# A two-layer conformer and attention trunk: the first layer's gated channels move one step ahead of queries and keys

## The chip, the cores and the metric

The kernel runs on one core of one Trainium2 chip. Its time is the device time of one execution in microseconds. Before the change three executions took 1055.93, 1056.01 and 1057.12 us; the median is 1056.01 us. One more execution was profiled: it took 1054.58 us, of which 1052.8 us lie between the first and the last instruction.

## The reference

Two layers work on 256 latent tokens and 256 context tokens of width 1024. Only the token-mixing half of the first layer matters here. Cut to that:

```python
h, hc = modulate(rmsnorm(x)), modulate(rmsnorm(xc))
p, pc = h @ w_in, hc @ w_in            # columns: GLU a | GLU g | q | k | v | gates
# convolution branch, 512 channels
u = a * sigmoid(g)
u = dwconv1d(u, dw, dw_b)              # 31 taps, each channel for itself
y_conv = silu(layernorm(u)) @ w_conv_out
# attention, 8 heads of 64: latent queries see a window of latent keys and all context keys,
# context queries see the context keys alone
y_attn = merge_heads(softmax(q @ k.T * scale + bias) @ v) @ w_na_out
# gated sum, and the residual add
x = x + g1 * ((sigmoid(p_gate_c) * y_conv + sigmoid(p_gate_a) * y_attn) @ w_out)
```

In the first layer the context tokens go through all of it too; in the second only their keys and values are needed.

## The kernel before

**Storage and matmuls.** Activations lie transposed: channels on the 128 partitions, tokens along the free axis (256 latent, then 256 context). Every weight is split into a high part and a remainder, and so is every activation, and a product is three matmuls (`mm3`, lines 196 to 199): high by high, high by low, low by high. A weight unit is 128 by 1024 values and makes one *group*: 8 blocks of 128 by 3 matmuls, 24 matmuls of 512 columns that add up in one PSUM bank. The high part is a cast on ScalarE (ACT). The remainder is either a subtraction on VectorE (DVE, line 168) or, for the units listed in `ADDED`, a DMA that adds in flight, issued by GpSimd (POOL, line 218). There are 8 PSUM banks: 4 named `main` for groups, 2 `sc`, 1 `pt` and 1 `po` (line 72).

**Slots and side work.** `group` calls `slot()` twice in a group of 512 columns, in the middle and at the end. A slot lets each generator in the list `side` take one step. Two of them matter: `conv_run` emits `rate[0]` taps of the depthwise convolution (one DVE instruction of 128 by 512 a tap, line 673), and `Attention.run` calls `Attention.step`, which decides by its count of slots whether a part of the attention is emitted now. `conv_run` is first in the list.

**Order of instructions.** The program order is a priority. The compiler's scheduler walks through it with its own estimate of durations and puts onto each engine the earliest instruction in program order that is ready. The order on each engine is then fixed, and the engine takes its instructions strictly in that order. `issue_after` adds an edge: a tap that is emitted after the scores of an attention block stands behind the last row maximum of that block (`after`, lines 516 and 660). So the taps emitted before a block may be placed ahead of its maxima, and the later ones may not.

**The convolution.** Channels are worked in four chunks j = 0 to 3. `glu(j)` (line 687) multiplies the two GLU groups of a chunk (a tanh on ACT, line 691, and one DVE instruction, line 693) and appends its 31 taps to the list. The taps of one chunk form a chain through the accumulator `cb[j]`. After the attention, `layer_norm` (line 938) emits what is left of the taps at 5 a slot, adds the chunks (lines 949 to 951), forms the mean with a matmul five slots later (line 955), and so on.

**Queries, keys and attention.** `qk(j)` (line 843) makes a group of queries and a group of keys for a pair of heads, turns them by the rotary tables on DVE (lines 859 to 869) and splits them (881 on ACT, 882 on DVE). With each pair one latent block is queued, and with each second pair one context block. A block passes three stages: `issue` (the score matmuls, line 495, the row maxima on DVE, 516, exponentials on ACT, 519, and their scaling, 522), `turn` (transposes on TensorE, 561, copies on ACT, 564 and 567) and `values` (578 and 587). `ahead(j)` forces steps until no block with a pair up to j is waiting to be issued, and returns the last copy of a `turn` in those steps. `glu_groups(j)` (line 701) makes the two GLU groups of a chunk, calls `ahead`, and lets `glu(j)` stand behind that copy.

**Stages of the first layer around the change.** The values and chunk 0 of the convolution come first. Then line 840 sets 2 taps a slot, and the program goes through queries and keys of pair 0, and for j = 1, 2, 3 the GLU groups of chunk j and queries and keys of pair j, at 3 taps a slot from j = 2 on. Up to five gate groups (line 708, a tanh each) follow while attention is busy, then empty slots until it is done. The other gate groups come after that, with the tiles of the pool `ec`, whose storage the attention held: among them the buffers `own` for the products of the modulation rows (`ada_dots`, line 304, 48 DVE instructions of 128 by 1024 in this stage). Both output projections of the branches follow, and `w_out`.

The second layer has its own order in the same lines, chosen by `last`.

Of the kernel before, what the change touches and what calls it, by code (L numbers as in the profile page):

```python
# [53 lines left out]
def trunk(ctx: ExitStack, tc: tile.TileContext, xt, cvec, crow, wall, wada, params, bias_t, rope_t, out):  # L54
# [13 lines left out]
    def nm(s):  # L68
        uid[0] += 1
        return f"{s}_{uid[0]}"  # L70
# [3 lines left out]
    def psum(tag="main"):  # L74
        return psp.tile([P, 512], F32, tag=tag, bufs=BANKS[tag], name=nm(tag))

    def tmp(w=512):
        return tp.tile([P, w], F32, tag="t", bufs=5, name=nm("t"))
# [10 lines left out]
    def add_side(gen):  # L89
        side.append(gen)  # L90

    def slot():
        for g in list(side):
            try:
                next(g)
            except StopIteration:
                side.remove(g)
# [79 lines left out]
    def wunit(l, u, at=None, cuts=1):  # L177
        w, more = wparts(l, u, at, cuts)
        more()
        return w  # L180
# [8 lines left out]
    def back(ps):  # L189

        return ps.rearrange("p (c r) -> p r c", r=2)

    def halves(a):
        return a.rearrange("p (r c) -> p r c", r=2)
# [403 lines left out]
    def blocks(ap):  # L598
        return ap.rearrange("p (r b c) -> p b r c", r=ROWS, b=NB_)
# [32 lines left out]
    for l in range(DEPTH):  # L632
        last = l == DEPTH - 1
# [4 lines left out]
        with ExitStack() if last else start as e1a:  # L638
# [36 lines left out]
            rate = [0.0]  # L675

            def conv_run():
                due = 0.0
                while True:
                    due += rate[0]  # L680
                    while due >= 1:
                        due -= 1
                        if taps:
                            conv_tap(*taps.pop(0))
                    yield

            def glu(j, pa, pg):
                while taps and taps[0][0] <= j - NU_:
                    conv_tap(*taps.pop(0))
                sg = tmp()  # L690
                act.activation(halves(sg[:, :T]), back(pg[:, :T]), AF.Tanh, scale=0.5)
                u = us[j % NU_][:, :, PAD : PAD + S]
                dve.scalar_tensor_tensor(
                    halves(u[:, 0]) if NS == 1 else u, halves(sg[:, :T]), 1.0, back(pa[:, :T]), ALU.add, ALU.mult
                )
                taps.extend((j, t) for t in range(TAPS))

            def in_group(t, c, tag="main"):
                return group(psum(tag), unit8(l, U_IN + t), *h1, c)

            def glu_groups(j):
                pa = in_group(T_GLU + 2 * (j - 1), ALL)
                pg = in_group(T_GLU + 2 * (j - 1) + 1, ALL)
                copied = None if last else att.ahead(j - 2)
                with tc.issue_after(copied.ins) if copied else ExitStack():
                    glu(j, pa, pg)

            def gate(pool_, n):
                ps = in_group(T_GATE + n, ALL)
                g = new_gate(pool_, n)  # L710
                act.activation(halves(g), back(ps[:, :T]), AF.Tanh, scale=0.5)

            with ExitStack() as e1b:
# [3 lines left out]
                att = Attention(l, eb, T, V, VW, oh, ol, after)  # L717

                def keep_v(t, ps):
                    if t > 1:  # L720
                        act.copy(halves(V[t - 2]), back(ps))
                        return
                    v = tmp()
                    act.copy(halves(v), back(ps))
                    for b in range(NB_):
                        for r in range(2):
                            at = r * GW + BASE[b]
                            sp.dma_start(VW[2 * t + r :: ROWS, b], v[at : at + WC])  # L728
# [108 lines left out]
                    glu_groups(1)  # L837

                conv = conv_run()
                rate[0] = 3 if last else 2.0  # L840
                add_side(conv)

                def qk(j):

                    att.ahead(j - 2)
                    bt = eb.tile([P, 5, NS_ // 2], F32, tag="bias", bufs=2 if last else 1, name=nm("bias"))
                    both = []
                    for what in range(2):
                        w = T if what == 0 else 2 * S
                        sc = HD ** -0.5 if what == 0 else 1.0  # L850
                        ps = in_group((T_Q, T_K)[what] + j, slice(0, w))
                        if what == 0:
                            with tc.issue_after(lastdma[0].ins):
                                sp.dma_start(bt, bias_t[l, j])
                        r1, r2 = tmp(), tmp()
                        got = back(ps[:, :w])
                        lat, ctx_ = (got[:, 0], got[:, 1]) if w > S else (got, None)
                        part = halves if w == S else lambda a: a
                        dve.tensor_tensor(part(r1[:, LAT]), lat, part(rope[:, 0, :]), ALU.mult)
                        dve.stream_shuffle(part(r2[:, LAT]), lat, SWAP16)  # L860
                        dve.tensor_tensor(r2[:, LAT], r2[:, LAT], rope[:, 1, :], ALU.mult)
                        if what == 0:
                            rq = tmp()
                            dve.tensor_tensor(
                                rq[:, LAT].rearrange("p (b r c) -> p b r c", b=NB_, r=ROWS),
                                blocks(r1[:, LAT]), blocks(r2[:, LAT]), ALU.add,
                            )
                        else:
                            dve.tensor_tensor(r1[:, LAT], r1[:, LAT], r2[:, LAT], ALU.add)
                        f = eb.tile([P, 2, KN if what else w], F32R, tag="qk"[what], bufs=2, name=nm("qk"))  # L870
                        if what == 0:
                            to = [([f[:, a, LAT] for a in range(2)], rq[:, LAT])]
                            if T > S:
                                to.append(([f[:, a, CTX] for a in range(2)], ctx_))
                        else:
                            rv_ = r1[:, LAT].rearrange("p (r c) -> p r c", r=ROWS)
                            to = [([f[:, a, KCTX] for a in range(2)], ctx_)]
                            for d, c in ((slice(0, KL), slice(GW - TC, GW)), (slice(KX, KN), slice(0, TC))):
                                to.append(([f[:, a, d].rearrange("p (c r) -> p r c", r=ROWS) for a in range(2)], rv_[:, :, c]))
                        for (hi, lo), src in to:  # L880
                            act.activation(hi, src, AF.Identity, scale=sc)
                            end = dve.scalar_tensor_tensor(lo, src, sc, hi.bitcast(F32), ALU.mult, ALU.subtract)  # L882
                        both.append(f)
                    att.pair(j, *both, bt, end)

                if l == 0:
                    for t in range(4):
                        keep_v(t, pv[t])
                    qk(0)
                    arun = att.run()  # L890
                    add_side(arun)
                    for j in range(1, 4):
                        glu_groups(j)
                        qk(j)
                        rate[0] = 3
                else:
                    glu_groups(2)
                    rate[0] = 3
                    wvs = [wunit(l, U_V + uu) for uu in range(4)]
                    for half in range(2):  # L900
                        pv = {t: psum() for t in (2 * half, 2 * half + 1)}
                        for k in range(KD):
                            v_tile(pv, wvs[k // 2], k, pv)
                            if k % 2:
                                slot()
                        for t, p in pv.items():
                            keep_v(t, p)
                    qk(0)
                    glu_groups(3)
                    arun = att.run()  # L910
                n = 0
                if last:
                    add_side(arun)
                    for j in range(1, 4):
                        gate(ea, n)
                        n += 1
                        qk(j)
                while att.busy() and n < (14 if last else 5):
                    gate(ea, n)
                    n += 1  # L920
                while att.busy():
# [435 lines left out]
```

## Time and profile before

| | |
|---|---|
| median of three executions | 1056.01 us (1055.93 to 1057.12) |
| profiled execution | 1054.58 us |
| its span, first to last instruction | 1052.8 us |
| TensorE matmul (PE) busy | 1032.4 us, 98% |
| DVE busy | 893.2 us, 85% |
| ACT busy | 565.6 us, 54% |
| mean granted TensorE clock | 0.997 |
| last matmul of chunk 0 issued, first tap | 56.0 us, 58.6 us |
| last tap of the first layer | 211.5 us |

A line of the profile's timeline has a start, a duration, the engine, the line of the kernel, the operation, what it writes and reads, its shape and a count; in brackets stands the idle time of the engine before it and what ended that. A line of the table of stretches has, after the stretch, its length and the busy time of each engine in it. Matmuls are pipelined and their ends are modelled, so a busy PE can still lose a little between two starts.

### The profile page before, as it was taken

How to read it: one execution, taken by the hardware profiler on the slowest of the kernel's cores; microseconds unless marked ns; L12 is line 12 of the kernel's file. 1: busy time of each engine (PE TensorE's matmuls, PEld its weight loads, DVE VectorE, ACT ScalarE, POOL GpSimd, SP SyncE). 2: the span in 40 equal slices, each digit the busy share in tenths (PEclk: the TensorE clock that was granted, in tenths of full speed). 3: DMA queues.
4: the chain of work that ended last, by engine and by line, in shares of the span. 5: the costliest groups of instructions: out<-in, count | busy, mean ns of one | idle time of the engine just before them, and what ended most of it. 6: DMA issues, size and time to landing. Idle time of an engine off the chain costs nothing.

```text
span 1052.8 us, 17991 instructions
## 1 busy us (share of the span) xinstructions
PE 1032.4 (98%) x6886; PEld 932.9 (89%) x6886; DVE 893.2 (85%) x1608; ACT 565.6 (54%) x921; POOL 43.7 (4%) x59
## 2 busy tenths in 40 slices
PE   9999999999999999999999999999999999999997
PEld 7787788888889988888888889999889999999996
DVE  6568899999998787878788888799899988988883
ACT  4458768545434644444444223545777666766652
POOL 1111110011000000000000000000000000000000
PEclk9999999999999999999999999999999999999998
DMA  9989674888945345454545887556734485666781
GB/s 374 305 221 229 156 181 121 258 255 236 305 146 177 104 140 160 140 164 143 166 145 160 301 289 249 180 189 209 208 123 135 161 292 176 193 201 199 221 283 57
DMA packets 59511, 209.26 MB, mean 199 GB/s; under 512 B 7201, under 2 KB 7457, under 8 KB 59425
## 3 DMA queue, kind: packets, MB, share of 16 engines
q1 hardware_dynamic: 54384, 190.77, 55.3%
q0 software_dynamic: 4752, 17.30, 8.7%
q8 instruction: 54, 0.88, 0.3%
q14 instruction: 33, 0.26, 0.1%
q10 hardware_dynamic: 288, 0.04, 0.0%
HBM read 187.63 MB, written 1.05 MB: 179 GB/s over the span
## 4 chain that ended last, share of the span: by engine, by line
PE 68%; DVE 17%; ACT 5%; DMA 4%; issue 3%; SPq 1%; DVEq 0%; ACTq 0%
PE main L197 20%; PE main L198 20%; PE main L199 20%; DVE cb L673 6%; PE main L736 4%; DVE wlo L168 3%; DMA raw<-in_wall 2%; DVE t L304 2%; DMA own<-in_wada 1%; SPq L728 1%; PE sc L197 1%; PE sc L199 1%; PE sc L198 1%; DVE qk L882 1%; ACT pp L519 1%
## 5 line engine op out<-in xcount | busy, mean ns | idle before, releaser
L197 PE MATMUL main<-h,whi 128*128 128x256 f32 (+1 forms) x1328 | 433.1, 326 | 1.2 <-DVE qk L882 1.2
L198 PE MATMUL main<-h,whi 128*128 128x256 f32 (+1 forms) x1328 | 430.2, 324 | 0.9 <-DVE h L1001 0.7
L199 PE MATMUL main<-h,wlo 128*128 128x256 f32 (+1 forms) x1328 | 429.9, 324 | 1.2 <-DVE wlo L168 1.1
L167 ACT CAST whi<-raw 128x1024 fp32r<-128x1024 f32 (+1 forms) x211 | 218.3, 1039 | 234.8 <-PE main L198 173.6
L168 DVE TENSOR_TENSOR wlo<-raw,whi 128x1024 fp32r<-128x1024 f32 (+1 forms) x211 | 253.6, 1208 | 67.2 <-ACT whi L167 66.4
L197 PEld LDWEIGHTS main<-h,whi 128*128 128x128 f32 x1328 | 252.8, 190 | 22.0 <-issue 1.3
L199 PEld LDWEIGHTS main<-h,wlo 128*128 128x128 f32 x1328 | 252.5, 190 | 18.5 <-DVE wlo L168 1.8
L198 PEld LDWEIGHTS main<-h,whi 128*128 128x128 f32 x1328 | 252.7, 190 | 18.3 <-DVE h L1001 1.0
L304 DVE CUSTOM_DVE_ANT_0 t<-own,sb,par 128x1024 bf16<-128x1024 f32 x120 | 151.8, 1282 | 6.8 <-DMA own<-in_wada 6.8
L673 DVE SCALAR_TENSOR_TENSOR cb<-u,par,cb 128x512 f32<-128x512 f32 (+1 forms) x240 | 144.7, 620 | 2.8
L198 PE MATMUL main<-fl,whi 128*128 128x256 f32 (+1 forms) x396 | 122.8, 310 | 0.0
L197 PE MATMUL main<-fh,whi 128*128 128x256 f32 (+1 forms) x396 | 122.8, 310 | 0.0
L199 PE MATMUL main<-fh,wlo 128*128 128x256 f32 (+1 forms) x396 | 122.5, 310 | 0.0
L197 PEld LDWEIGHTS main<-fh,whi 128*128 128x128 f32 x396 | 75.6, 191 | 3.8 <-ACT fh L1095 0.2
L198 PEld LDWEIGHTS main<-fl,whi 128*128 128x128 f32 x396 | 75.6, 191 | 3.7 <-DVE fl L1096 0.2
L199 PEld LDWEIGHTS main<-fh,wlo 128*128 128x128 f32 x396 | 75.5, 191 | 3.6
L216 ACT CAST whi<-raw 128x1024 fp32r<-128x1024 f32 x33 | 34.6, 1049 | 36.0 <-PE main L198 30.5
L404 ACT ACTIVATE h<-t,mod 128x256 fp32r<-128x256 f32 x56 | 25.2, 503 | 34.8 <-DVE t L403 34.3
L218 POOL DMA_DIRECT2D wlo<-raw x33 | 28.9, 877 | 258.9 <-ACT wlo L217 107.6
L736 PE MATMUL main<-whi,h 128*128 128x512 f32 x128 | 38.5, 386 | 0.2
L1105 ACT ACTIVATE t<-t 128x512 f32<-128x512 f32 x22 | 13.9, 632 | 41.3 <-DVE t L1074 41.3
L217 ACT ACTIVATE wlo<-whi 128x1024 fp32r<-128x1024 f32 x33 | 35.0, 1061 | 0.5
(214 smaller groups left out, 1268.8 us busy)
## 6 DMA issues: line engine op xcount, KB each, us to landing
raw<-in_wall SPq DMA_DIRECT2D x240, 512.0 KB, 4.3
own<-in_wada SPq DMA_DIRECT2D x72, 512.0 KB, 4.7
wlo<-raw POOLq DMA_DIRECT2D x33, 512.0 KB, 5.4
raw<-in_wada SPq DMA_DIRECT2D x16, 512.0 KB, 5.8
bias<-in_bias_t SPq DMA_DIRECT2D x8, 520.0 KB, 5.3
row<-in_wada SPq DMA_DIRECT2D x8, 512.0 KB, 5.1
sb<-in_crow SPq DMA_DIRECT2D x5, 512.0 KB, 4.8
x<-in_xt SPq DMA_DIRECT2D x4, 512.0 KB, 5.1
```

The costliest lines, as they stand in the source:

```text
L167: act.copy(hi[:, c], r[:, c])
L168: dve.tensor_tensor(lo[:, c], r[:, c], hi[:, c].bitcast(F32), ALU.subtract)
L197: pe.matmul(ps, w[0], order(xh), start=start, stop=False)
L198: pe.matmul(ps, w[0], order(xl), start=False, stop=False)
L199: pe.matmul(ps, w[1], order(xh), start=False, stop=stop)
L216: act.copy(hi, r)
L217: act.mul(lo, hi.bitcast(F32), -1.0)
L218: pool.dma_start(lo, r, accum_op=ALU.add)
L304: dve.tensor_tensor_reduce(tmp().bitcast(BF16), r, v, 1.0, pr(l, BADA + n, 1), ALU.mult, ALU.add, mods[l][:, n, s : s + 1])
L404: high = act.activation(hi[:, c], y[:, c], AF.Identity, bias=b)
L673: dve.scalar_tensor_tensor(cb[j], src, w, cb[j], ALU.mult, ALU.add)
L736: mm = pe.matmul(pv[t], h1[n == 1][k][:, c], runs(w[n == 2][:, b]), start=k + n == 0, stop=k == KD - 1 and n == 2)
```

## The change

In the first layer each chunk of the convolution now comes one step earlier than the queries and keys that it stood beside. Chunk 1 comes ahead of pair 0, chunk 2 ahead of pair 1, chunk 3 ahead of pair 2, and a gate group stands in the old place of chunk 3, ahead of pair 3. `glu_groups` asks for one pair less (`j - 3`). The convolution goes at 4 taps a slot from the start. Up to 8 gate groups, counted with the one ahead of pair 3, may follow while attention is busy. The second layer keeps its order and its 3 taps a slot; it has its own limits in the shared lines.

```diff
             def glu_groups(j):
                 pa = in_group(T_GLU + 2 * (j - 1), ALL)
                 pg = in_group(T_GLU + 2 * (j - 1) + 1, ALL)
-                copied = None if last else att.ahead(j - 2)
+                copied = None if last else att.ahead(j - 3)
                 with tc.issue_after(copied.ins) if copied else ExitStack():
                     glu(j, pa, pg)
...
                 conv = conv_run()
-                rate[0] = 3 if last else 2.0
+                rate[0] = 3.0
                 add_side(conv)
...
                 if l == 0:
                     for t in range(4):
                         keep_v(t, pv[t])
+                    rate[0] = 4.0
+                    glu_groups(1)
                     qk(0)
                     arun = att.run()
                     add_side(arun)
-                    for j in range(1, 4):
-                        glu_groups(j)
+                    for j in range(1, 3):
+                        glu_groups(j + 1)
                         qk(j)
-                        rate[0] = 3
                 else:
...
                 n = 0
                 if last:
                     add_side(arun)
-                    for j in range(1, 4):
+                for j in range(1 if last else 3, 4):
+                    if True:
                         gate(ea, n)
                         n += 1
                         qk(j)
-                while att.busy() and n < (14 if last else 5):
+                while att.busy() and n < (14 if last else 8):
                     gate(ea, n)
                     n += 1
                 while att.busy():
```

## The prediction

> **What bounds the kernel now.** I read the page first.
>
> ```profile
> span 1052.8 us, 17991 instructions
> PE 1032.4 (98%) x6886; PEld 932.9 (89%) x6886; DVE 893.2 (85%) x1608; ACT 565.6 (54%) x921; POOL 43.7 (4%) x59
> ```
>
> TensorE is busy for 98% of the span, and the change takes no matmul away. So all that can be won is TensorE's idle time. The table of stretches, cut at the attention's blocks, shows how much of that lies where the change works.
>
> ```profile
> core 0: us, PE busy (x) PEld busy (x) DVE busy (x) ACT busy (x) POOL busy (x), PEclk, DMA share, GB/s
> 58.00:90.00 32.00, 32.00 (x174) 27.48 (x173) 24.52 (x55) 21.55 (x34) 4.80 (x7) 1.00 0.94 239
> 90.00:126.00 36.00, 34.02 (x242) 28.30 (x243) 31.98 (x74) 28.35 (x66) 5.11 (x6) 1.00 0.68 164
> 126.00:152.00 26.00, 24.27 (x154) 20.61 (x148) 25.64 (x57) 16.98 (x32) 3.46 (x4) 1.00 0.79 181
> 152.00:187.00 35.00, 34.80 (x281) 27.81 (x278) 31.73 (x60) 28.81 (x68) 1.97 (x3) 1.00 0.49 127
> 187.00:213.00 26.00, 25.05 (x117) 21.59 (x115) 25.05 (x38) 12.74 (x16) 2.40 (x3) 1.00 0.93 284
> 213.00:250.00 37.00, 36.98 (x175) 32.16 (x176) 33.42 (x52) 19.64 (x28) 4.52 (x4) 1.00 0.82 248
> 250.00:316.00 66.00, 65.34 (x329) 57.26 (x328) 64.10 (x110) 25.19 (x34) 3.62 (x5) 1.00 0.76 228
> ```
>
> Length less PE busy is, stretch by stretch, 0, 1.98, 1.73, 0.20, 0.95, 0.02 and 0.66 us: 5.5 us in all. The list of TensorE's waits says whom it waited for.
>
> ```profile
> PE sc L495 <- ACT pT L567: 1.7, 1, 1.7
> PE po L955 <- DVE ss L951: 1.0, 1, 1.0
> PE sc L495 <- ACT qk L881: 0.9, 1, 0.9
> PE main L198 <- DVE h L1001: 0.7, 1, 0.7
> PE sc L495 <- DVE qk L882: 0.6, 1, 0.6
> ```
>
> Three waits stand at score matmuls (line 495): for the keys of pair 1, split on ACT and DVE (0.9 and 0.6), and for transposed probabilities (1.7). One stands at the mean of the layer norm (1.0), behind the last taps, and one at the inputs of `w_out`. DVE is busy for 89 to 99% of every stretch in which TensorE waited. So DVE decides, and the question is what stands ahead of what in its queue.
>
> **Rate against pace.** The unit is a group:
>
> ```profile
> 56.20 0.38 PE L197 MATMUL main<-h,whi 128*128 128x512 f32 x1
> ...
> 61.38 0.38 PE L197 MATMUL main<-h,whi 128*128 128x512 f32 x1
> ```
>
> 24 matmuls from 56.20 to 61.38 are 5.18 us, a slot 2.59 us. Next, DVE's timeline:
>
> ```profile
> 59.19 3.12 DVE L673 SCALAR_TENSOR_TENSOR cb<-u,par,cb 128x512 f32<-128x512 f32 x4
> 62.22 0.42 DVE L859 TENSOR_TENSOR t<-main,rope 128x256 f32<-128x256 f32 x1
> ...
> 62.90 0.74 DVE L673 SCALAR_TENSOR_TENSOR cb<-u,par,cb 128x512 f32<-128x512 f32 x1
> 63.55 0.42 DVE L861 TENSOR_TENSOR t<-t,rope 128x256 f32<-128x256 f32 x1
> ...
> 72.25 2.30 DVE L673 SCALAR_TENSOR_TENSOR cb<-u,par,cb 128x512 f32<-128x512 f32 x3
> 77.84 0.60 DVE L516 CUSTOM_DVE_ANT_0 sc<-sc,bias 128x416 f32<-128x416 f32 x1 [3.29 <-PE sc L495]
> ...
> 80.60 0.69 DVE L693 SCALAR_TENSOR_TENSOR u<-t,main 128x512 f32<-128x512 f32 x1 [1.55 <-ACT t L691]
> 83.56 0.16 DVE L521 RECIPROCAL ri<-sm 128x1 f32<-128x1 f32 x1 [2.27 <-ACT pp L519]
> ...
> 96.91 2.33 DVE L673 SCALAR_TENSOR_TENSOR cb<-u,par,cb 128x512 f32<-128x512 f32 x3
> 99.16 0.59 DVE L516 CUSTOM_DVE_ANT_0 sc<-sc,bias 128x416 f32<-128x416 f32 x1
> ...
> 135.65 4.06 DVE L673 SCALAR_TENSOR_TENSOR cb<-u,par,cb 128x512 f32<-128x512 f32 x6
> ```
>
> Four taps of one chain in a row start every (3.12 - 0.75) / 3 = 0.79 us; a tap with a rotary instruction behind it takes 0.65 (62.90 to 63.55); six taps that alternate between two chunks start every (4.06 - 0.76) / 5 = 0.66 us. Four taps a slot are thus 2.6 to 3.2 us of DVE in 2.59 us of TensorE, before any other work: the new rate alone fills DVE.
>
> [...]
>
> **What a second chunk in hand gives.** Before, only 16 taps may stand ahead of the first maximum (8 slots at 2). DVE has done them by 74.55 and then idles 3.29 + 1.55 + 2.27 = 7.1 us. Now 12 slots at 4, 48 taps, may, and DVE has work there. That is gained on DVE, not on TensorE, whose idle time from 58 to 90 is 0, and chunk 1's groups only change places with others of the same length.
>
> **The keys and the softmax of pair 1 (1.98 us now).** This is where I see the price. From the first tap (58.60, just ahead of the row at 59.19) to the first maximum of pair 1 (99.16) DVE needs 40.6 us, and all 30 taps allowed there (8 slots at 2, 4 at 2, 2 at 3) stand ahead of it: the row at 96.91 is the last three. After the change chunk 1's groups and the slots up to this block, 18 at 4, allow 72. If all of them stand ahead again: 42 more taps by 0.66 are 27.7, one more `u` (0.69) is added, 7.1 of idle time goes: 40.6 + 27.7 + 0.7 - 7.1 = 61.9, and the maximum starts at 58.6 + 61.9 = 120.5. TensorE's score matmuls come two groups later than now:
>
> ```profile
> 96.04 0.44 PE L495 MATMUL sc<-qk,qk 64*128 64x416 f32 x2 [0.87 <-ACT qk L881]
> 97.07 0.62 PE L495 MATMUL sc<-qk,qk 64*128 64x416 f32 x4 [0.58 <-DVE qk L882]
> ...
> 104.94 1.08 PE L578 MATMUL po<-pT,V 128*64 128x256 f32 x8
> 105.85 0.63 PE L587 MATMUL po<-pT,VW 128*64 128x64 f32 x16
> ```
>
> And the last scaling of the softmax, on ACT:
>
> ```profile
> 103.26 1.29 ACT L522 ACTIVATE pp<-pp,ri 128x416 f32<-128x416 f32 x2
> ```
>
> Without the wait of 0.87 the scores start at 95.2, so after the change at 95.2 + 10.4 = 105.6. The transposes need the last scaling, which ends 103.26 + 1.29 - 99.16 = 5.4 us after the first maximum: at 125.9. Meanwhile TensorE has the twelve score matmuls (some 1.2, as four take 0.62 and partly overlap), one GLU group (5.2), the values of pair 0 (104.94 to 106.48, 1.5) and the queries of pair 2 (5.2): until 118.7. Further it can't go: of the four `main` banks one holds scores, two the GLU groups of chunk 3, which wait for a copy of this very `turn` (line 705), and one the queries, whose rotary work stands behind the taps too. The upper bound is an idle time of 7.2 us. The lower one is none: maxima may alternate with taps as rotary work does at 62.22 to 63.89. Between the two I go by the row at 135.65, where two chunks' taps alternate and let nothing between, but for part of the taps only, since chunk 1's are nearly used up by then: 3.0 us in place of 1.98, **+1.0**. Queued behind the maxima on DVE are the rotary work of pair 2 and `u` of chunk 3; on ACT, behind the exponentials, casts of weights.
>
> **The scores of pair 2 (1.73 us).**
>
> ```profile
> 125.32 0.81 ACT L881 ACTIVATE qk<-t 128x160 fp32r<-128x160 f32 x2 [1.58 <-DVE t L869]
> 125.91 1.07 ACT L216 CAST whi<-raw 128x1024 fp32r<-128x1024 f32 x1
> 127.02 1.06 ACT L217 ACTIVATE wlo<-whi 128x1024 fp32r<-128x1024 f32 x1
> 127.98 1.05 ACT L567 COPY pT<-sc 128x512 f32<-128x512 f32 x2
> ```
>
> ACT waited 1.58 us for keys from DVE, and two weight conversions of 1.07 and 1.06 then stood ahead of the copies that TensorE wanted. After the change one group still lies between keys and scores: a gate group in place of half of chunk 3. This gate brings a tanh on ACT that was there for the GLU anyway and takes a `u` off DVE. The stall is an accident of ACT's order. It can vanish (-1.73) or, with DVE later, double (+1.7). I take **-0.7**: the rate's taps are more, but the queue is laid out anew.
>
> **The end of the attention and the layer norm (0.20 and 0.95 us).**
>
> ```profile
> L951 DVE TENSOR_TENSOR ss<-ss,cb 128x512 f32<-128x512 f32 x1 | 0.7, 693 | 0.0
> ```
>
> The slots up to the first gate behind the last keys number 31, and 31 by 4 is all 124 taps. So none are left for `layer_norm`, whose sums come in its first slot and whose mean comes five slots, 13 us, later: the wait of 0.95 goes, **-0.95**; nothing is next in line, since three sums of 0.7 fit into 13 us. The 0.20 stay. Six gates in place of five cover the last blocks after the last keys, so no slot is empty.
>
> **Modulation rows.**
>
> ```profile
> 196.55 1.28 DVE L304 CUSTOM_DVE_ANT_0 t<-own,sb,par 128x1024 bf16<-128x1024 f32 x1 [0.60 <-DMA own<-in_wada]
> ```
>
> And the taps that DVE still did after 196 (a stretch of line 673 alone):
>
> ```profile
> 196.00:213.00 17.00, 6.75 (x9) 1.00 0.96 301
> ```
>
> The DMAs of the rows wait for storage that the attention holds, and attention now ends about two groups (10.4 us) later in TensorE's work, as 21 groups come up to its end where 19 did. The 9 taps, by 0.66 5.9 us, are now done earlier. DVE loses 10.4 - 5.9 = 4.5 us against 316. Its idle time from 213 to 316 is 3.58 + 1.90 = 5.5 us, which just covers that: **0**. Were the cover gone, up to 4.5 us would show at `w_out`'s inputs; at best the 0.66 there go. POOL's additions and SP's weight loads keep their order but for two units moved past two others, and TensorE never waits for a weight in this stage: 0.
>
> **Sum.** 1.0 - 0.7 - 0.95 + 0 = -0.65. On the profiled time, 1054.58 - 0.65 = 1053.93. The median lies 1.43 above the profiled time, which gives **1055.4 us**. Measurement can tell some 0.2%, 2.1 us, from no change.
>
> **Rivals.**
>
> *Faster:* the scheduler lets maxima between the taps, and DVE's regained 7.1 us keep keys and softmax ahead. Then the waits at 126 to 152 and in the layer norm go, and half of the 1.98: -1.73 - 0.95 - 1.0 = -3.7, 1052.3 us. For it speaks the alternation at 62.22; against it, that all 30 allowed taps stand ahead of the maximum at 99.16.
>
> *Slower:* all allowed taps lead, and TensorE stands 7.2 us before the transposes of pair 1, for want of a bank: 7.2 - 1.98 - 0.95 = +4.3, 1060.3 us. It decides from 72 allowed taps by 0.66: each tap fewer ahead of the maxima takes 0.66 off, and at 61 the idle time is gone. For it speak DVE's 89 to 99%, and 2.6 us of taps in a slot of 2.59.
>
> *Nothing:* the scheduler places taps by readiness, not rate, and the order comes out much as before: 1056.0 us.
>
> **How the numbers follow.** The forecast, stalls traded one for another, within -2.5 and +2: 0.35. Faster rival: 0.33. Slower: 0.28. Nothing: 0.04. Of the forecast's share 0.04 lie beyond 2.1 us on the fast side, and of the fast rival's 0.01 within: faster 0.36, same 0.36, slower 0.28. The range takes in both rivals, the faster one with the 0.66 at `w_out` and 1.1 more out of the 1.98 and 0.20 (1050.5), and the slower one with a little of the 4.5 at the modulation rows (1061.5). Outside lie the full 4.5 on top of it, and all of the 5.5 us won. The forecast's own range is 1053.5 to 1058.
>
> **What would show it.** In the profile after: DVE without its idle 7.1 us around 75 to 84 (if not, the first step is wrong); more than 60 taps ahead of pair 1's first maximum, and an idle time of TensorE of about 3 us there, at scores or transposes; no wait at line 955; the last tap some 15 us or more ahead of the last attention values; the first product of line 304 near 207. An idle time above 5 us at pair 1 would make the slower rival right; waits at scores of under 1.5 us in all, the faster one.

## The result, and the profile after

The change makes the kernel slower. Its median is 1072.27 us (five runs, 1071.17 to 1076.29) against 1056.01 before (five runs, 1055.44 to 1057.12); the ratio is 1.0162, with a 95% interval of 1.0142 to 1.0183. The forecast was 1055.4, with a range of 1050.5 to 1061.5. The profiled execution of after took 1072.27 us with a span of 1070.5; 17.7 us of span separate the two profiles.

The page of after, first lines. TensorE has the same number of matmuls and is busy 7.2 us longer, though no work was added to it:

```profile
span 1070.5 us, 17984 instructions
...
PE 1039.6 (97%) x6886; PEld 936.0 (87%) x6886; DVE 888.8 (83%) x1608; ACT 564.7 (53%) x921; POOL 43.4 (4%) x59
```

Two cuts show where the time went: the first product of the branches (its input is `oh`) and the first product that reads the hidden layer (`fh`). The part from the first tap of line 673 to the one holds attention and all 16 gates; the part from there to the other holds the branches, `w_out`, and then norm 2 and the up-projection, with which the feed-forward half of the layer begins. The table of stretches of before, cut there:

```profile
58.60:246.40 187.80, 182.92 (x1109) 154.24 (x1108) 168.22 (x325) 123.91 (x234) 21.15 (x23) 1.00 0.77 205
246.40:562.97 316.57, 315.91 (x1645) 281.31 (x1644) 270.87 (x422) 143.47 (x195) 5.75 (x7) 1.00 0.54 166
```

And of after, with four stretches from inside the first part. After the length come PE, PEld, DVE, ACT and POOL busy, then the granted TensorE clock:

```profile
60.03:259.68 199.65, 188.58 (x1107) 157.49 (x1106) 161.96 (x321) 123.70 (x234) 21.11 (x23) 0.97 0.72 189
259.68:579.74 320.06, 317.23 (x1645) 281.40 (x1644) 273.06 (x426) 143.26 (x195) 5.74 (x7) 1.00 0.55 166
88.00:108.00 20.00, 18.60 (x111) 15.51 (x110) 19.89 (x46) 15.40 (x28) 2.58 (x3) 1.00 0.85 213
108.00:120.00 12.00, 7.81 (x23) 4.35 (x23) 12.00 (x24) 3.63 (x7) 1.75 (x2) 0.72 0.76 176
120.00:132.00 12.00, 8.05 (x76) 6.60 (x77) 9.87 (x24) 8.64 (x20) 0.86 (x1) 0.93 0.41 96
174.00:212.00 38.00, 37.79 (x280) 31.24 (x281) 17.51 (x39) 26.21 (x63) 1.73 (x2) 1.00 0.47 127
```

The first part is 11.85 us longer, the second 3.49; the first tap comes 1.43 later, and what follows 579.74 takes 0.93 more (490.76 against 489.83). That adds up to 17.7. The 1.43 is no price of the change: kernels with the same code up to there have their first tap anywhere from 58.7 to 60.0.

Of the 11.85, TensorE's idle time makes 11.07 - 4.88 = 6.2, and 188.58 - 182.92 = 5.7 are busy time stretched by a granted clock below 1 (0.72 from 108 to 120). DVE shows the pattern behind both: full from 108 to 120 while TensorE stands, and idle for 38.00 - 17.51 = 20.5 us from 174 to 212. The taps were done so early that nothing was left for DVE there, and the early ones stood in the way of what TensorE wanted. The list of TensorE's waits in after, 58 to 350 us (in total, how many, the longest):

```profile
PE pt L495 <- ACT qk L881: 4.2, 1, 4.2
PE sc L561 <- ACT pp L522: 3.2, 2, 2.5
PE sc L495 <- DVE qk L882: 1.7, 2, 1.4
PE sc L495 <- ACT qk L881: 1.2, 1, 1.2
PE pt L561 <- ACT pp L522: 0.7, 1, 0.7
```

The 4.2 us are for pair 1's keys, the 3.2 and 0.7 for its scaled probabilities. DVE's timeline in after shows why both are late:

```profile
103.29 0.41 DVE L861 TENSOR_TENSOR t<-t,rope 128x256 f32<-128x256 f32 x1
103.62 0.74 DVE L673 SCALAR_TENSOR_TENSOR cb<-u,par,cb 128x512 f32<-128x512 f32 x1
104.29 0.41 DVE L864 TENSOR_TENSOR t<-t,t 128x256 f32<-128x256 f32 x1
104.62 0.74 DVE L673 SCALAR_TENSOR_TENSOR cb<-u,par,cb 128x512 f32<-128x512 f32 x1
...
106.62 2.06 DVE L673 SCALAR_TENSOR_TENSOR cb<-u,par,cb 128x512 f32<-128x512 f32 x3
108.60 0.41 DVE L859 TENSOR_TENSOR t<-main,rope 128x256 f32<-128x256 f32 x1
...
114.97 6.70 DVE L673 SCALAR_TENSOR_TENSOR cb<-u,par,cb 128x512 f32<-128x512 f32 x10
121.60 0.59 DVE L516 CUSTOM_DVE_ANT_0 sc<-sc,bias 128x416 f32<-128x416 f32 x1
...
182.67 0.73 DVE L673 SCALAR_TENSOR_TENSOR cb<-u,par,cb 128x512 f32<-128x512 f32 x1
...
217.51 1.28 DVE L304 CUSTOM_DVE_ANT_0 t<-own,sb,par 128x1024 bf16<-128x1024 f32 x1 [7.53 <-DMA own<-in_wada]
```

A tap of 0.67 stands between any two steps of the rotary work (0.34 each), so that a step starts every 1.0 us and queries and keys take three times as long; three taps run ahead of the keys' first step, and ten ahead of the first maximum. The last tap is the one at 182.67, 25 us ahead of attention's last values (207.9). The first modulation row comes at 217.51; its storage is free only when attention ends.

### The profile page after: what moved, and what is told of

Read it like the earlier page. It is cut to its first block, busy times and chain, and to the rows that moved or that the text cites. A ratio compares the mean times of both kernels' runs of the same rounds, so it can differ in the third digit from the quotient of the medians.

```text
span 1070.5 us, 17984 instructions
## 1 busy us (share of the span) xinstructions
PE 1039.6 (97%) x6886; PEld 936.0 (87%) x6886; DVE 888.8 (83%) x1608; ACT 564.7 (53%) x921; POOL 43.4 (4%) x59
## 4 chain that ended last, share of the span: by engine, by line
PE 69%; DVE 20%; ACT 4%; DMA 3%; issue 2%; SPq 1%; DVEq 0%; POOL 0%; ACTq 0%; POOLq 0%
PE main L197 20%; PE main L198 20%; PE main L199 20%; DVE cb L673 6%; PE main L736 3%; DVE wlo L168 3%; DMA raw<-in_wall 2%; DVE t L304 2%; SPq L728 1%; DVE qk L882 1%; ACT pp L519 1%; PE sc L199 1%; PE sc L198 1%; PE sc L197 1%; DVE t L403 1%
```

## The experiments

Theory R: the rate is the price. Too many taps may lead pair 1's keys and maxima. Theory O: the order is, with gated chunks a step ahead, more gates and a later end of attention. Before, run beside them, had medians of 1055.59 to 1057.07 us; each ratio in brackets is to the runs of before beside that kernel. Taps "by the program" are counted in the order in which DVE's instructions are issued.

**Rate against order.** `a_rates23` is after with before's rates, `a_rate3` is after with 3, `b_rate4` is before with 4 throughout (its expectation lets three follow behind pair 1, but the edit takes out that line too).

```diff
 a_rates23:
-                    rate[0] = 4.0
+                    rate[0] = 2.0
                     glu_groups(1)
...
                         qk(j)
+                        rate[0] = 3.0
 a_rate3:
-                    rate[0] = 4.0
+                    rate[0] = 3.0
 b_rate4 (on before):
-                rate[0] = 3 if last else 2.0
+                rate[0] = 3 if last else 4.0
...
-                        rate[0] = 3
```

> The kernel after with its order of products and its gates kept, but two taps a slot in layer 0 until the last queries and keys are issued ahead of pair 1's end of the loop, and three from then on (as before had it). Theory R (the rate is the price: taps allowed ahead of pair 1's keys and maxima make DVE late, TensorE idles over 3.4 us there and its granted clock halves for 10.2 us): no half-clock stretch, the 4.35 us idle at pair 1's scores falls below 2 us, and the time is 1054 to 1059 us. Theory O (the order is the price: gated chunks ahead, a chunk ahead of the last keys, more gates and an attention stage that ends later): 1066 us or more. In between, both pay.

> The kernel after with three taps a slot instead of four throughout layer 0. By the program some 44 taps stand ahead of the rotary work of pair 1's keys and 52 ahead of its first maximum, between the 24 and 30 of before and the 53 and 69 of after. Theory R: about half the loss or less, 1055 to 1064 us, idle at pair 1's scores 0 to 3 us and no half-clock stretch. Theory O: 1066 us or more.

> The kernel before with its order kept and four taps a slot from the start of layer 0's run of taps to the end of pair 1 (there three follow as before). 39 and 47 taps stand ahead of pair 1's keys' rotary work and first maximum, 15 and 17 more than before. Theory R: slower than before by 2 to 12 us, with TensorE idle over 2 us at pair 1's scores or transposes. Theory O: 1054 to 1058 us.

They gave 1063.05 (1.0063, 1.0044 to 1.0081), 1062.68 (1.0054, 1.0039 to 1.0069) and 1066.87 us (1.0089, 1.0072 to 1.0106). By time `a_rate3` and `b_rate4` lie where theory R had them (`a_rate3` with some 3.4 us at half clock that it did not expect: 0.50 from 110.7 to 114.0 us), and `a_rates23` lies between the two. Neither theory alone fits: against before's median beside them (1057.07), four taps cost 9.8 us in before's order, and the new order with its gates 6.0 at before's rates. The stretches of `a_rates23` separate them.

```profile
58.90:244.38 185.48, 182.35 (x1108) 154.11 (x1106) 163.95 (x314) 120.80 (x228) 21.09 (x23) 1.00 0.74 200
244.38:571.68 327.30, 319.59 (x1647) 284.58 (x1645) 276.97 (x432) 146.75 (x201) 5.75 (x7) 0.98 0.55 165
```

In the first part the new order is no loss: with two and three taps a slot it takes 185.48 us, 2.3 less than before, with 3.1 us of idle time. So what after lost there comes of the rate, the only thing in which the two differ. The order, with its gates, pays in the second part: 10.7 us. `b_rate4` is the mirror image: 197.59 and 316.84. Its waits name the same place, and pair 3's keys besides (the 4.2, at 163 us), which four taps a slot lead there too:

```profile
PE pt L495 <- ACT qk L881: 6.5, 2, 4.2
PE pt L561 <- ACT pp L522: 1.3, 2, 0.8
```

**Is it the halved clock?** In after the granted clock stands at 0.5 from 113.2 to 120.0 and from 130.3 to 133.7. Extra products of no use were put where TensorE waits, so that it isn't idle, while DVE's work stays what it was.

```diff
 a_warm12 (22 in a_warm22_12), in products, first layer, (j, qt) == (1, 0):
+                for _ in range(12):
+                    pe.matmul(out[0], h1[0][0][:, :P], h1[0][0][:, : 2 * S], start=True, stop=True)
 a_warm22_12 also, in turn, pair 1, n == 0: 12 of them into banks[0]
 a_r23warm44 (on a_rates23), ahead of the first products of the hidden layer:
+                for _ in range(44):
+                    pe.matmul(pss[0][:, CTX], first[0][0][0], z[0][0][:, CTX], start=True, stop=True)
```

> The kernel after with twelve extra products of 512 columns put into the bank of pair 1's first scores just ahead of them; the scores overwrite what they leave, so the output is what it was. They can run while TensorE waits for pair 1's keys and cost nothing where they fit into that wait. If the half-clock stretches come from that idle and carry a part of the loss, the stretch of 0.5 at 113 us is gone and the time falls to 1066 to 1070 us; if the clock stays at 0.5 or costs nothing (other engines set the time there), it stays at 1072 within 1.5 us.

> The kernel after with 22 extra products of 512 columns ahead of pair 1's first scores and 12 ahead of pair 1's transposes, in banks that are written again before they are read; 4.7 and 2.6 us at 0.213 us each, about what TensorE stands there (4.35 us and 4.5 us). If the half clock is what makes much of the loss at pair 1, the clock is whole between 100 and 135 us and the time falls by 3 to 5 us, to 1067 to 1069 us. If DVE's lateness alone sets the pace there, the clock is whole and the time stays within 1.5 us of 1072.

> a_rates23 (the order of after, two and three taps a slot) with 44 extra products of 256 columns put ahead of the first products of the hidden layer, into columns of the first bank that are written again before they are read. Their 4.9 us (44 by 0.111) fit into the 5.4 us that TensorE waits there for weight lows of DVE, so the wait's end stays where it was and only TensorE's idle time goes. If the half-clock stretch of 10.24 us at 335 us follows from the idle time and costs time, it is gone and the run is shorter by 3 to 5 us: 1058 to 1060 us. If DVE sets the pace there whatever the clock: 1062 to 1064 us, though the clock stays whole.

`a_warm12` gave 1072.38 us (1068.23 to 1073.05), `a_warm22_12` 1074.41 (1070.29 to 1077.47), `a_r23warm44` 1061.81 (1061.27 to 1063.18). In `a_warm12` the granted clock is still 0.93 from 100 to 125 us and 0.98 over the first part, and so it answers only in part. The stretches of `a_warm22_12`:

```profile
59.67:259.18 199.51, 192.02 (x1141) 161.05 (x1140) 162.12 (x321) 124.05 (x234) 21.15 (x23) 1.00 0.70 189
108.00:132.00 24.00, 19.52 (x140) 15.01 (x140) 23.86 (x50) 12.13 (x25) 2.21 (x3) 1.00 0.62 148
```

The clock is whole, and yet the first part takes 199.51 us where after took 199.65, and the median is no better. DVE is busy for 23.86 of 24 us, and pair 1's first maximum starts 61.3 us after the first tap, as in after (61.6). So DVE's queue sets that time, whatever the clock. This does not show that the halved clock is free. Pair 1's transposes start 65.7 us after the first tap where after has 67.5, and the twelve products end just where they begin, so that they may hide some gain. `a_gates5` below has the instructions of after in the same order up to there, but a lower granted clock, 0.95 over its first part against 0.97, and its scores of pair 2 start 95.1 us after the first tap where after has 93.2. In `a_r23warm44` the clock is whole in the second part too (1.00, where `a_rates23` has 0.98), which falls from 327.30 to 324.76 us; on the medians that is 1.2 us, less than the 3 to 5 expected. In both places the clock rose when products filled the idle time (0.97 to 1.00 over the first part, 0.98 to 1.00 over the second), and by these runs it is a price of some 2 us at each place, not the loss.

**What the second part loses.** In `a_rates23` TensorE waits 5.4 us from 333 us on for weight lows, the remainders of weights that line 168 makes. That wait, and DVE's timeline ahead of it:

```profile
PE sc L199 <- DVE wlo L168: 5.4, 1, 5.4
```

```profile
321.53 1.28 DVE L304 CUSTOM_DVE_ANT_0 t<-own,sb,par 128x1024 bf16<-128x1024 f32 x1
...
326.35 1.28 DVE L304 CUSTOM_DVE_ANT_0 t<-own,sb,par 128x1024 bf16<-128x1024 f32 x1
...
327.56 0.15 DVE L378 TENSOR_SCALAR red<-pt 128x2 f32<-128x2 f32 x1
327.63 0.47 DVE L1010 SCALAR_TENSOR_TENSOR x<-main,mod,x 128x256 f32<-128x256 f32 x1
```

Five modulation rows (one instruction of line 304 each) that were left over are made in one go, 6.0 us, ahead of the residuals and norm 2; this is the *lump* below. `pace[0]` is how many rows become due in a slot. Theory G: a gate more inside attention starts the rows later and leaves less between attention and the branches (60.8 us in before, 51.8 in after and in `a_rates23`), so that rows are left over. Theory L: the rows' loads or something else of the order. By the trace five gates end inside attention in before, six in after.

```diff
 a_g5r23 (on a_rates23), a_gates5 (on after):
-                while att.busy() and n < (14 if last else 8):
+                while att.busy() and n < (14 if last else 5):
 b_gates8 (on before): the reverse
 a_r23pace7 (on a_rates23), behind attention:
-                    pace[0] = 0.5
+                    pace[0] = 0.7
```

> The order of after with the two and three taps a slot of before (as in a_rates23) and, besides, at most five gates beside attention, as before has, instead of eight. a_rates23 came to the first product of the branches 2.0 us ahead of before (244.4 against 246.4) and to the first product of the hidden layer 8.7 us behind it (571.7 against 563.0), with 51.8 us instead of 60.8 between the last values of attention and the branches. Theory G (a gate more inside attention takes away slots in which the modulation rows are made; DVE has them left over for norm 2, where TensorE then stands 5.6 us and drops to half clock): the span from the last values to the branches is back above 56 us, no half clock near 335, 1053 to 1059 us. Theory L (the loads of the modulation rows, or what else of the order comes late, not the gates): 1061 us or more.

> The kernel after with four taps a slot kept and at most five gates beside attention instead of eight. Theory R and G together (the rate's price lies ahead of pair 1, the gates' price behind attention): the idle time and half clock at 108 to 134 us stay, and the loss behind 280 us (some 3.5 us in after) goes: 1066 to 1070 us. If gates are not a price here: 1071 to 1074 us. If they carry most of the loss: below 1063 us.

> The kernel before with up to eight gates beside attention instead of five, nothing else. Theory G: a gate or so moves from behind attention into it, the rows of the modulation run into norm 2, and it is slower than before by 2 to 9 us, with the loss between 267 and 345 us. Theory L: within 1.5 us of before.

> a_rates23 with the pace of the modulation rows behind attention raised from 0.5 to 0.7 a slot until the branches begin, all else as there. Theory G: rows move ahead of the branches, the stall at 333 us goes, and the time falls from 1063 to 1054 to 1060 us. Theory L: the rows' loads do not come faster (DMA shares of 0.96 to 0.98 stood at 198 to 222 us), DVE waits for them, TensorE's banks are freed later, and it is 1062 us or more.

They gave 1066.08 us, 1072.58, 1056.79 (ratio 0.9999, 0.9982 to 1.0017) and 1062.39. By total times theory G fails in all four, yet in the three that change the gates its own quantity moves as it says. The second part of `a_g5r23` and its wait in the first:

```profile
257.56:575.07 317.51, 316.28 (x1645) 281.25 (x1644) 270.71 (x422) 143.21 (x195) 5.75 (x7) 1.00 0.54 166
```

```profile
PE po L958 <- DVE ss L954: 6.0, 1, 6.0
```

The late loss is gone (327.30 to 317.51), and so is it in `a_gates5` (320.06 to 316.64); `b_gates8` gains one (316.57 to 318.63). What is won is given back in the first part. With the gate outside, attention's end has less to cover it: TensorE's waits for the context blocks' scaled probabilities (line 540) are 1.4 us in `a_gates5` and none in after, 2.3 in `a_g5r23` and 1.0 in `a_rates23`. In `a_g5r23`, whose taps end at 221 us, TensorE also waits 6.0 us for the layer norm's mean. `a_gates5` goes from 199.65 to 205.70; of these 6.05 us some 1.9 are there by the scores of pair 2 and are put down to the lower clock (0.95 against 0.97), which the gates did not bring. `a_r23pace7` hardly did what it was meant for: two rows come earlier (215.2 instead of 223.8 us), but 18 stand ahead of the branches as in `a_rates23`, and the lump stays as it was (five rows, the same wait at 333 us). Its time lies in theory L's range, but DVE waits for no row's load in it; it tells nothing of the two theories.

**Lump or load.** Two kernels only spread the left-over rows, and one brings the taps forward late in attention.

```diff
 a_r23co5 (on a_rates23), a_co5 (on after):
-                pace[0] = 0.0 if last else 0.3
+                pace[0] = 0.0 if last else 0.5
 a_r234 (on a_rates23), behind the last keys:
+                if not last:
+                    rate[0] = 4.0
```

> a_rates23 with the pace of the modulation rows beside the second branch raised from 0.3 to 0.5 a slot. By the program that takes the lump of rows that is made all at once ahead of norm 2 from five to one (before has one, after three). If the lump carries the late loss: no wait for weight lows at 333 us, no half clock there, 1054 to 1057 us. If the loss comes of DVE's whole load between 190 and 330 us, the rows moved ahead hold up the branch instead: 1060 us or more.

> The kernel after with nothing changed but the pace of the rows beside the second branch, 0.5 instead of 0.3: the lump ahead of norm 2 falls from three rows to one. The idle time and the half clock between 108 and 134 us stay. If the lump carries the late loss of after (some 3 us between 280 and 580 us): 1068 to 1070.5 us; if not, 1072 within 1.5 us.

> a_rates23 with four taps a slot behind the last keys: the taps end earlier without leading any keys, and by the program the lump ahead of norm 2 falls from five rows to three. A lump of three went with some 2.5 us of idle time near 340 us and little half clock in other runs, so by the lump theory 1056 to 1060 us; 1062 us or more if the lump is not what costs.

`a_r23co5` gave 1058.74 us: the wait at 333 us and its halved clock are gone (1.00 over the second part against 0.98), and with them 4.3 us; 1.0026 (1.0011 to 1.0042) of before is left, and its second part is 321.16 us, still 4.6 longer than before's. `a_co5` gave 1074.87, no gain at all, with waits of 2.4 us where `w_out` begins and its inputs come late (until 307 us), and of 1.1 for the reader of a bank at 312. `a_r234` gave 1067.65: the extra taps lead the last maxima (98 instead of 92 ahead of the last block), and its first part grows from 185.48 to 191.09. Its lump falls to three rows as expected, and the wait for weight lows from 5.4 to 0.6 us, yet the second part is 327.55 us, as long as in `a_rates23` (327.30). So the lump is only one form that the late loss takes: rows moved out of norm 2 delay the inputs of `w_out` in after, and in `a_r234` the idle time lies elsewhere. That DVE's whole load behind attention is the common cause is likely, but no run shows it by itself.

**How many taps may lead.** The last kernels keep after's order and raise the rate only until pair 0's keys; `b_early3` does that in before's order.

```diff
 a_early4 (a_early3: 3.0; a_early3co5: also the 0.5 of a_r23co5; a_g5early3: also five gates), on after:
                     rate[0] = 4.0
                     glu_groups(1)
                     qk(0)
+                    rate[0] = 2.0
...
                         qk(j)
+                        rate[0] = 3.0
 b_early3 (on before):
-                rate[0] = 3 if last else 2.0
+                rate[0] = 3.0
...
                     qk(0)
+                    rate[0] = 2.0
```

> The order of after with four taps a slot only until pair 0's queries and keys are issued, two until pair 1's and three from there. By the program 48 taps stand ahead of pair 1's keys (after 53, a_rates23 33) and 54 ahead of its first maximum (after 69, a_rates23 38). DVE stood idle for 7.8 us between 72 and 96 us in a_rates23, time for 11 taps of 0.7 us; 15 more therefore make the keys some 3 us late: an idle of 2 to 4 us at pair 1's scores, none over 1.5 us at its transposes, 1060 to 1066 us. If only the taps between the keys and the maxima were the price: 1056 to 1060 us, no idle over 2 us at the scores.

> As a_early4, with three taps a slot until pair 0's keys instead of four: 40 taps ahead of pair 1's keys and 46 ahead of its first maximum, seven more than a_rates23, which fit into the 7.8 us that DVE stood idle there. No idle over 1.5 us at pair 1's scores or transposes; the taps end some 5 us earlier than in a_rates23 (210); the lump ahead of norm 2 is five rows by the program as there, so the stall and half clock at 333 us stay: 1060 to 1064 us.

> a_early3 with the pace of the modulation rows beside the second branch 0.5 instead of 0.3, which takes the lump ahead of norm 2 from five rows to one. a_r23co5 gained 4.3 us by that on a_rates23. If what was left of the loss there (1058.7 against 1055.6) is DVE's load behind attention, the seven taps done earlier relieve it by 5 us: 1053 to 1057 us. If it is something else in the order: 1058 to 1061 us.

> a_early3 with at most five gates beside attention instead of eight. From the first tap to the branches a_early3 took 185.7 us (before 187.8), from there to the first product of the hidden layer 326.4 (before 316.6); kernels with five gates inside attention took 316.6 to 317.5 for the second part, whatever their taps did. a_g5r23 paid for it with 6.2 us of waiting for the convolution's mean, since its last tap came at 221 us; here the seven taps done earlier put it near 210 and the wait below 2 us. If that account is right: 186 to 190 and 316 to 318, in all 502 to 508 against 504.4, that is 1054 to 1060 us. If the late loss hangs on something else of the order: 1061 us or more.

> The order of before with three taps a slot, instead of two, until pair 0's queries and keys are issued, two until pair 1's and three from there: the change's thought alone, to use DVE's idle time ahead of pair 0's softmax, with 29 and 34 taps ahead of pair 1's keys and first maximum (before 24 and 30, after 53 and 69). DVE's idle of 7.1 us there takes some five taps of 0.7 us without making pair 1 late. If the account by idle time is right: TensorE's idle time from the first tap to the branches 13 to 16 us (before 15.0), the second part 316 to 318 us, 1053 to 1058 us. If these five taps already make pair 1's keys or maxima late: 1059 us or more.

They gave 1062.33, 1064.31 (0.3 above its range), 1060.59, 1058.17 (ratio 1.0013, 0.9996 to 1.0030) and 1061.35 us (1.0053, 1.0031 to 1.0075). Together with the others, cut at the same two places (length, and idle time as length less PE busy). The parts are those of one profiled execution, which for `a_r23co5` was the fastest of ten (1056.41) and for `a_r234` the slowest of four (1069.78):

| kernel | median us | first part | idle | second part | idle |
|---|---|---|---|---|---|
| before | 1056.01 | 187.80 | 4.88 | 316.57 | 0.66 |
| b_gates8 | 1056.79 | 188.00 | 4.16 | 318.63 | 2.19 |
| b_early3 | 1061.35 | 189.25 | 5.30 | 322.00 | 2.81 |
| b_rate4 | 1066.87 | 197.59 | 8.72 | 316.84 | 0.87 |
| a_g5early3 | 1058.17 | 190.96 | 6.02 | 317.36 | 1.54 |
| a_r23co5 | 1058.74 | 185.43 | 3.09 | 321.16 | 4.53 |
| a_early3co5 | 1060.59 | 184.91 | 2.10 | 324.74 | 6.40 |
| a_early4 | 1062.33 | 188.93 | 4.72 | 322.77 | 4.02 |
| a_rate3 | 1062.68 | 189.41 | 4.67 | 321.84 | 3.09 |
| a_rates23 | 1063.05 | 185.48 | 3.13 | 327.30 | 7.71 |
| a_early3 | 1064.31 | 185.74 | 2.93 | 326.38 | 7.33 |
| a_g5r23 | 1066.08 | 197.59 | 10.71 | 317.51 | 1.23 |
| a_r234 | 1067.65 | 191.09 | 4.27 | 327.55 | 6.75 |
| after | 1072.27 | 199.65 | 11.07 | 320.06 | 2.83 |
| a_gates5 | 1072.58 | 205.70 | 12.57 | 316.64 | 0.87 |
| a_co5 | 1074.87 | 200.21 | 10.51 | 323.73 | 4.11 |

Three things follow. First, in after's order and with its gates the first part grows with the taps ahead of pair 1's first maximum: 38 and 46 (`a_rates23`, `a_early3`) give 185.5 and 185.7 us, 52 and 54 (`a_rate3`, `a_early4`) 189.4 and 188.9, 69 (after) 199.65. Some eight taps more than at before's rates are free there, as DVE's idle time would have it, and those beyond cost. The count alone does not decide: in before's order 34 taps (`b_early3`) cost 1.5 us against 30, and `b_rate4` has 197.6 with 47, though part of that is pair 3's wait. The waits at pair 1's scores in `a_early4` were 0.9 + 0.6 = 1.5 us where 2 to 4 were expected. Second, taking the gate limit back to five shortened the second part in all three pairs (after 3.4, `a_rates23` 9.8, `a_early3` 9.0 us) and raising it in before lengthened it by 2.1. The account of `a_g5early3` came out in the second part and missed the first by 1 us, with 2.1 us of waiting for the mean. Third, no kernel beats before. The best first part (184.91) and the best second (316.57) were never had together. In after's order, what lets the first part run, a gate more inside attention, is what makes the second late. `a_early3co5`, with that best first part and the rows spread, then stands 6.4 us (4.7 and 1.7) where `w_out` begins. `b_early3` spoils even the second: four taps brought forward raise the wait for pair 1's keys on ACT from 0.9 to 2.0 us and bring one of 1.8 at the inputs of `w_out`, which I had not expected. Why its second part is 5.4 us longer with five gates inside attention stays open. That `glu_groups` asks for one pair less was not tried by itself.

## Why the prediction was wrong

- **DVE's 7.1 us of idle time around 75 to 84 is regained**: right but for 2.1 us (81.94, a wait for ACT's split of a query).
- **More than 60 taps lead pair 1's first maximum**: right. 69 do, and the maximum starts 121.60 - 60.03 = 61.6 us after the first tap, where the upper case was worked out at 61.9. That it fits so well is luck in part: three taps fewer than 72 take 2.0 us off, and the 2.1 us of idle time that stayed put them back.
- **3.0 us of idle time, +1.0**: this step failed. It set the lower end at none, since maxima may alternate with taps, and took a value between. With 69 taps leading, the upper end was the case at hand. The waits at pair 1 are 4.2 + 3.2 + 0.7 = 8.1 us, above even the 7.2 of the bound.
- **The scores start at 105.6**: wrong within that step. Only the maxima were counted as queued behind taps. The keys were too: 53 taps stand ahead of their rotary work, so that the scores start at 112.6, and TensorE stands ahead of the scores first (4.2 us) and again ahead of the transposes.
- **The scores of pair 2, -0.7**: 1.2 us of waiting stay of 1.7, and pair 0's scores, which had no wait, have one of 1.4.
- **No wait at the mean, -0.95**: right, line 957 of after has none.
- **Modulation rows, 0**: wrong by some 3.5 us, the growth of the second part. The step assumed that attention ends 10.4 us later and that 4.5 us on DVE can be made up. It ended 22 us later, the first row came at 217.5 instead of 207, and DVE had stood idle before that for lack of taps. The 4.5 given as the cost without cover is near what was measured. With five gates (`a_gates5`) the growth is gone.
- **The slower rival** had the mechanism, with the right decider (taps ahead of the maxima), and 1060.3 us. It lacked the keys, credited the waits of before as saved, and held the rest of the kernel unmoved. The price was not one stall but the whole first part: DVE, full from 84 to 120 us (busy for 35.89 of 36) with taps ahead of what TensorE waited for, set the pace, and its time was given back unused between 174 and 212.
- **0.66 us a tap**: right where chains alternate: in after the ten taps from 114.97 on start every 0.66 us, the first thirteen, of one chain, every 0.79.

The argument that TensorE could win 5.5 us at most is contradicted by no run, and the new order with slower taps did win 2.3 us in the first part (`a_rates23`).

## What to carry to other kernels

Count what a filler leads, not how much of it fits: work that nobody waits for must be rationed by what stands behind it in its engine's queue, each step of the keys as well as the softmax, and the filler's time saved early is worth nothing if the engine has none left later. When a trace gives the number of instructions that will stand ahead, take the case that it gives, not the middle of the range. Cut a kernel's time at two or three fixed products and compare the parts: a change can win in one and lose more in the next, and a total hides both.

## What the runs showed of the hardware

TensorE's granted clock drops to half inside a kernel that is busy for 97% of its span. The stretches of after (its table of stretches; the clock stands behind POOL's busy time):

```profile
113.20:120.00 6.80, 6.80 (x20) 3.87 (x18) 6.80 (x12) 1.54 (x2) 0.87 (x1) 0.50 0.78 217
130.30:133.60 3.30, 3.30 (x30) 3.08 (x29) 2.82 (x5) 2.33 (x7) 0.00 (x0) 0.50 0.62 194
```

In the trace's clock record these stretches are 6.83 and 3.41 us long, with 10.24 us of whole clock between them. Products of 512 columns start 0.43 us apart in the first (118.48 and 118.91 us) and 0.21 to 0.22 apart behind it (120.11, 120.32 and 120.54). The busy share does not show them: 20 matmuls fill 6.8 us, and PE counts as busy throughout. How much idle time comes ahead of one differs, and no run shows an amount that brings one on. The one at 113.2 us in after follows a wait of 4.2 us. In `a_early4` 1.48 us of idle time in 6.4 us were followed by one, while in before 1.45 in 6.0 were not:

```profile
104.00:110.40 6.40, 4.92 (x28) 3.67 (x28) 6.33 (x14) 5.41 (x10) 0.88 (x1) 1.00 0.57 102
110.60:113.90 3.30, 3.30 (x9) 2.67 (x8) 3.08 (x12) 1.98 (x6) 0.69 (x1) 0.50 1.07 246
```

```profile
92.00:98.00 6.00, 4.55 (x27) 3.46 (x25) 5.93 (x14) 5.32 (x10) 0.86 (x1) 1.00 0.71 171
```

Ten runs of `a_early4` lie between 1058.23 us at a mean clock of 0.998 and 1066.93 at 0.993. Whether the clock makes those runs longer, or idle time both, was not tried. What the clock is worth shows best in two comparisons: `a_gates5`, with 0.95 over its first part against 0.97, comes to the scores of pair 2 1.9 us later than after, and the second part of `a_r23warm44`, with 1.00 against 0.98, is 2.5 us shorter than that of `a_rates23`.
